# RMSNorm on one core: the first tile's store is cut in two, the last tile's load is put ahead of the second tile's store, and that store goes out as one transfer

## The chip, the cores and the metric

The kernel runs on one core of a Trainium2 chip. The metric is the device time of one execution in microseconds (us); a "span" in a profile is shorter by about 2 us, because it runs from the first to the last instruction. The time before was 162.24 us (median of 3 runs, 161.93 to 162.32).

## The reference

```python
def reference(x, gamma):            # x: 16 x 1024 x 512 float32, gamma: 512 float32
    eps = 1e-5
    rms = np.sqrt(np.mean(x ** 2, axis=-1, keepdims=True) + eps)
    return (x / rms * gamma).astype(np.float32)
```

The input is 33.55 MB and so is the output. Each must cross once between HBM (the memory outside the core) and SBUF (the core's working memory): 67.1 MB in all.

## The kernel before

The 16384 rows are cut into four tiles. In each tile a partition holds R = 32 consecutive rows of 512 floats, 2 KB each, so one tile is 64 KB per partition and 8.4 MB. Three tiles fit into SBUF (`slots`); tile 3 uses slot 0 again, so its load must wait until tile 0 has been stored. All large transfers are issued by the Sync engine (SP), on one queue that feeds 16 DMA engines. ACT (ScalarE) and VectorE (DVE in the profile) compute.

```python
slots = [const.tile([P, R, D], fp32, name=f"slot{i}") for i in range(3)]

def load(t, slot, r0, r1):
    nc.sync.dma_start(out=slots[slot][:, r0:r1], in_=xv[t][:, r0:r1])

def store(t, slot, r0, r1):
    nc.sync.dma_start(out=ov[t][:, r0:r1], in_=slots[slot][:, r0:r1])

load(0, 0, 0, 8)
load(0, 0, 8, 32)
# ... gamma is broadcast to gamma_b; row_stats(slot, g): ACT squares 8 rows,
# ... ACT or VectorE sums them, ACT takes the root, VectorE the reciprocal

def apply(slot, g, rstd):            # VectorE scales 8 rows in place
    for r in range(G):
        nc.vector.scalar_tensor_tensor(
            out=slots[slot][:, g + r, :], in0=slots[slot][:, g + r, :],
            scalar=rstd[:, r : r + 1], in1=gamma_b, op0=OP.mult, op1=OP.mult)

def transfers(t, g):                 # after group g of tile t has been scaled
    if (t, g) == (0, 0):
        store(0, 0, 0, 1)
        load(1, 1, 0, 32)
        load(2, 2, 0, 16)
        store(0, 0, 1, 2)
        load(2, 2, 16, 32)
    elif (t, g) == (0, 24):
        store(0, 0, 2, 32)
    elif (t, g) == (1, 8):
        store(1, 1, 0, 16)
        load(3, 0, 0, 16)
        load(3, 0, 16, 32)
    elif (t, g) == (1, 24):
        store(1, 1, 16, 32)
    elif (t, g) == (2, 24):
        store(2, 2, 0, 32)
    elif (t, g) == (3, 8):
        store(3, 0, 0, 16)
    elif (t, g) == (3, 24):
        store(3, 0, 16, 32)

ahead = row_stats(0, 0)
for k, (t, g) in enumerate(groups):  # statistics run one group ahead
    rstd = ahead
    # ... ahead = row_stats of the next group
    apply(slot_of[t], g, rstd)
    transfers(t, g)
```

## Time and profile before

| what | before |
|---|---|
| time, median of 3 runs | 162.24 us |
| span of the profile | 160.0 us |
| VectorE (DVE) busy | 122.6 us (77%) |
| ACT busy | 80.1 us (50%) |
| share of 16 DMA engines' time, Sync queue | 97.9% |
| first data packet starts, last one ends | 1.7 us, 158.8 us |
| VectorE's last instruction ends, last store is issued | 146.6 us |

The first fence is from the page of the kernel before: busy times, then the span in 40 slices of 4 us (busy tenths, and the GB/s that the DMA engines moved), the DMA queue, and the chain of work that ended last.

```profile
span 160.0 us, 409 instructions
...
PE 2.0 (1%) x2; PEld 0.5 (0%) x2; DVE 122.6 (77%) x163; ACT 80.1 (50%) x162; POOL 0.2 (0%) x4
...
DVE  0101928999999509999999999999999999996000
...
DMA  5999999699699999997999999999996996999993
...
q1 hardware_dynamic: 2160, 67.11, 97.9%
...
DVE 67%; DMA 14%; ACT 7%; issue 2%; DVEq 0%; SPq 0%
```

Two readings compete here. The chain gives VectorE 67%, which looks like a kernel that VectorE bounds. The queue line gives the DMA engines 97.9%. The chain ends in VectorE because the last store is released by VectorE; it does not show that this store then stands in a queue behind other stores. VectorE is at rest in the last slices while DMA is not.

The second fence holds the issues of the Sync engine in the timeline of the kernel before (start, length until the last of the merged issues ends, line, number). L45 is a store and L42 a load. The last row is the last store by itself, which the row above it also counts.

```profile
49.91 23.23 SPq L45 DMA_DIRECT2D out_dram<-slot  x2
...
81.86 1.19 SPq L42 DMA_DIRECT2D slot<-in_x_dram  x2
...
85.73 61.22 SPq L45 DMA_DIRECT2D out_dram<-slot  x4
...
146.62 0.33 SPq L45 DMA_DIRECT2D out_dram<-slot  x1
```

The third is the waits of the Sync engine's own queue: who waited, on what, us in total, times, longest.

```profile
SPq L45 <- DVE slot L88: 120.4, 7, 29.8
...
SPq L42 <- DMA out_dram<-slot: 8.6, 1, 8.6
```

The 8.6 us are the load of tile 3 waiting until tile 0 is stored. The change is aimed at this wait and at where the load stands.

A count can be made from the trace's record of every packet: at each moment, how many of the 16 engines had a packet in flight. I call the missing ones, summed over time and divided by 16, "idle engine time"; a stretch of it between two transfers, when the queue has run dry, is a "hole" ("bubble"). Some packets overlap, by about 0.4 us in all, so the idle time can be understated by as much. For the kernel before it is 0.9 us of 157.1 us between first and last packet: 0.2 us at the start, 0.6 us at the end when the engines finish one after the other, and almost nothing between. A packet of 32 KB takes 1213 ns and one of 64 KB 2418 ns, loads and stores alike.

### The profile page before, as it was taken

To read this page: it belongs to the slowest core of one execution; us is meant where nothing else is said; L and a number is where in the kernel's file an instruction comes from. 1 tells how busy PE (TensorE), PEld (TensorE's weight loads), DVE (VectorE), ACT (ScalarE), POOL (GpSimd) and SP (SyncE) were. 2 spreads that over 40 slices of the span, in tenths; PEclk is the share of its full clock that TensorE was granted. 3 is DMA by queue.
4 is the path that set the end of the run, shared out by engine and by line. 5 is a ranking of instruction groups with operands and counts; after the bars stand their busy time and mean duration, and the time that the engine had idled before them with its cause. 6 is when DMAs were issued, how large, how long until landed. Compare 5 with 4: busy or idle time off the path is not lost.

```text
span 160.0 us, 409 instructions
## 1 busy us (share of the span) xinstructions
PE 2.0 (1%) x2; PEld 0.5 (0%) x2; DVE 122.6 (77%) x163; ACT 80.1 (50%) x162; POOL 0.2 (0%) x4
## 2 busy tenths in 40 slices
PE   4000000000000000000000000000000000000000
PEld 1000000000000000000000000000000000000000
DVE  0101928999999509999999999999999999996000
ACT  3098029991291999996900960069709950000000
POOL 0000000000000000000000000000000000000000
DMA  5999999699699999997999999999996996999993
GB/s 197 524 393 393 430 487 508 279 524 491 295 395 396 456 467 434 494 461 323 445 393 475 426 410 426 475 410 410 491 524 295 508 491 295 467 434 410 426 475 147
DMA packets 2164, 67.13 MB, mean 420 GB/s; under 512 B 241, under 2 KB 241, under 8 KB 498
## 3 DMA queue, kind: packets, MB, share of 16 engines
q1 hardware_dynamic: 2160, 67.11, 97.9%
q14 instruction: 2, 0.02, 0.0%
q10 hardware_dynamic: 2, 0.00, 0.0%
HBM read 33.56 MB, written 33.55 MB: 419 GB/s over the span
## 4 chain that ended last, share of the span: by engine, by line
DVE 67%; DMA 14%; ACT 7%; issue 2%; DVEq 0%; SPq 0%
DVE slot L88 48%; DVE ss L71 18%; DMA slot<-in_x_dram 14%; ACT sq_scratch L76 3%; ACT sq L70 3%; DVE rstd L83 1%; ACT rms L82 1%; DVEq L155 0%; SPq L42 0%
## 5 line engine op out<-in xcount | busy, mean ns | idle before, releaser
L88 DVE SCALAR_TENSOR_TENSOR slot<-slot,rstd,gamma_b 128x512 f32<-128x512 f32 x128 | 85.8, 741 | 0.1
L76 ACT ACTIVATE sq_scratch<-slot 128x512 f32<-128x512 f32 x64 | 40.0, 625 | 10.0 <-DMA slot<-in_x_dram 8.7
L70 ACT ACTIVATE sq<-slot 128x2048 f32<-128x2048 f32 x16 | 29.8, 1865 | 18.8 <-DVE ss L71 11.5
L71 DVE TENSOR_REDUCE ss<-sq 128x4 f32<-128x2048 f32 x16 | 35.9, 2277 | 3.6 <-ACT sq L70 3.6
L82 ACT ACTIVATE rms<-ss,eps_t 128x8 f32<-128x8 f32 x16 | 4.6, 297 | 26.2 <-DVE ss L71 26.0
L83 DVE RECIPROCAL rstd<-rms 128x8 f32<-128x8 f32 x16 | 3.1, 196 | 16.3 <-ACT rms L82 16.3
L76 ACT ACTIVATION_READ_ACCUMULATOR sq_scratch<-slot 128x1 f32 x64 | 11.9, 186 | 0.0
L57 DVE COPY gamma_b<-sq 128x512 f32<-128x512 f32 x1 | 0.7, 691 | 3.3 <-PE sq L55 3.3
L55 PE MATMUL sq<-gamma_row,ones_col 1*128 1x512 f32 x2 | 2.0, 1122 | 2.2 <-DMA gamma_row<-in_gamma_dram 2.2
L76 ACT ACT_TABLE_LOAD x1 | 1.3, 1283 | 1.3 <-PEq L144 1.3
L82 ACT ACT_TABLE_LOAD x1 | 1.3, 1283 | 0.0
L53 DVE MEMSET ones_col<- 1x128 f32 x1 | 0.2, 165 | 0.8 <-PEq L144 0.8
L55 PEld LDWEIGHTS sq<-gamma_row,ones_col 1*128 1x128 f32 x2 | 0.5, 308 | 2.1 <-issue 2.1
L144 POOL MEMSET const-uint8-127<- 128x1 uint8 x1 | 0.1, 102 | 0.0
L144 POOL MEMSET const-bfloat16-1.0<- 128x1 bf16 x1 | 0.1, 101 | 0.0
L144 POOL MEMSET const-float32-0.0<- 128x1 f32 x1 | 0.1, 98 | 0.2 <-issue 0.2
L144 POOL MEMSET const-float32-1.0<- 128x1 f32 x1 | 0.1, 98 | 0.0
L60 DVE MEMSET eps_t<- 128x1 f32 x1 | 0.1, 59 | 0.0
## 6 DMA issues: line engine op xcount, KB each, us to landing
slot<-in_x_dram SPq DMA_DIRECT2D x4, 4096.0 KB, 32.1
out_dram<-slot SPq DMA_DIRECT2D x4, 4096.0 KB, 18.4
out_dram<-slot SPq DMA_DIRECT2D x1, 7680.0 KB
slot<-in_x_dram SPq DMA_DIRECT2D x1, 6144.0 KB, 21.6
slot<-in_x_dram SPq DMA_DIRECT2D x1, 2048.0 KB, 7.2
out_dram<-slot SPq DMA_DIRECT2D x2, 256.0 KB, 21.4
gamma_row<-in_gamma_dram ACTq DMA_DIRECT2D x1, 2.0 KB
slot<-in_x_dram SPq DMA_DIRECT2D x1, 25.9
```

Source lines behind the costliest of these rows:

```text
L53: nc.vector.memset(ones_col, 1.0)
L55: nc.tensor.matmul(gamma_psum[:, 0], ones_col, gamma_row, start=True, stop=True)
L57: nc.vector.tensor_copy(out=gamma_b, in_=gamma_psum[:, 0])
L60: nc.vector.memset(eps_t, eps)
L70: nc.scalar.activation(out=sq, in_=slots[slot][:, g + h : g + h + H, :], func=AF.Square)
L71: nc.vector.tensor_reduce(out=ss[:, h : h + H], in_=sq, axis=mybir.AxisListType.X, op=OP.add)
L76: nc.scalar.activation(out=sq_scratch, in_=slots[slot][:, g + r, :], func=AF.Square, accum_out=ss[:, r : r + 1],)
L82: nc.scalar.activation(out=rms, in_=ss, func=AF.Sqrt, bias=eps_t, scale=1.0 / D)
L83: nc.vector.reciprocal(out=rstd, in_=rms)
L88: nc.vector.scalar_tensor_tensor(out=slots[slot][:, g + r, :], in0=slots[slot][:, g + r, :], scalar=rstd[:, r : r + 1], in1=gamma_b, op0=O ...
L144: nc = _bacc.Bacc("TRN2", target_bir_lowering=False, num_devices=1)
```

## The change

The intent: load tile 3 as early as its slot allows. Tile 0's store is cut in two so that the first half of slot 0 is free while the second half is still being stored; the load of tile 3 follows directly, ahead of all of tile 1's store; tile 1 is then stored in one transfer with 64 KB rows.

```diff
         elif (t, g) == (0, 24):
-            store(0, 0, 2, 32)
-        elif (t, g) == (1, 8):
-            store(1, 1, 0, 16)
+            store(0, 0, 2, 16)
+            store(0, 0, 16, 32)
             load(3, 0, 0, 16)
             load(3, 0, 16, 32)
         elif (t, g) == (1, 24):
-            store(1, 1, 16, 32)
+            store(1, 1, 0, 32)
```

## The prediction

> **What bounds the kernel now.** The DMA engines. The table of DMA queues gives the Sync queue 97.9% of the time of 16 engines. The chain of waits ends in VectorE (67%), but VectorE is done at 146.6 us of a 160.0 us span (timeline). In the trace's packet records the first data packet starts 1.7 us and the last one ends 158.8 us after the start of the span: 157.1 us for 67.1 MB. Counted by packets in flight, the 16 engines lack only 0.9 us (mean of 16), nearly all at the start and in the last microsecond: no bubble in the middle. A 32 KB packet takes 1213 ns and a 64 KB one 2418 ns, loads and stores alike: 27.0 and 27.1 GB/s per engine, 434 GB/s for 16. The Trainium skill, "DMA: Bandwidth & Descriptors", section "Where 436 GB/s comes from", puts the ceiling of the SBUF ports at 435 GB/s; the trace agrees.
>
> **What the change does.** It removes no byte and adds no transfer: store of tile 0 becomes two (28 KB and 32 KB rows), store of tile 1 becomes one (64 KB rows instead of twice 32 KB). 15 transfers on the queue before and after. A 64 KB packet saves 8 ns of 2426, so 8 packets per engine save about 0.06 us. The work of ACT is in the same order; on VectorE one reciprocal in tile 3 moves behind one multiply, which may save 0.26 us.
>
> **Does the new order open a bubble?** As the same page says under "Anatomy of one DMA", waiting is done by the issuing sequencer and not by the DMA engines; what counts is whether the next transfer is issued before the queue runs dry. By the measured rates (us from span start):
> - first half of the remaining store of tile 0: runs 62.3 to about 71; the first load of tile 3 is issued at about 72, while the second half is stored (71 to 80.5). Slack 7 us.
> - second load of tile 3: issued at about 82 (as before, 81.9 to 83), while the first is running (80.5 to 90). Slack 7 us.
> - store of tile 1: waits for VectorE's end of tile 1 at 85.7; its turn is at about 100. Slack 14 us.
> - store of tile 2: issued at 115.9, turn at about 119.5, as before. The two of tile 3: issued at 131.5 and 146.6, turns at about 138.5 and 148.2, as before. The last has the least slack, some 0.5 us (issue to first packet took 1.0 us at the start).
>
> Tile 3 lands about 10 us earlier (about 90 and 100 instead of 100 and 110), but ACT first wants it at about 106, and the waits show no DMA wait after 43 us. So it releases nothing. The Sync queue's wait on tile 0's store (8.6 us) becomes two, some 22 and 9 us, both behind queued transfers.
>
> **Prediction.** 162.2 us, range 161.7 to 162.7. Faster by over 2%: 1%; within 2%: 98%; slower: 1%.
>
> **What would show it.** Right: Sync queue again near 98%, mean near 420 GB/s, last packet about 157 us after the first, VectorE's end at 146 to 147 us, no ACT wait on a load after 45 us, packet times unchanged. Wrong: a slice in which fewer than 16 packets are in flight near 72, 82, 100 or 148 us, or 64 KB stores slower than 2.42 us.
>
> **What would make it wrong.** VectorE ending later by over half a microsecond, or reads and writes beside each other slowing packets.

## More of the kernel before

Whether a wait of the Sync engine costs time depends on whether the DMA engines still have work queued meanwhile. The windows view of the kernel before answers that for the two critical moments (columns: window, its length, busy us of PE, PEld, DVE, ACT and POOL with counts, PE clock, DMA share, GB/s).

```profile
80.00:82.00 2.00, 0.00 (x0) 0.00 (x0) 2.00 (x5) 0.17 (x2) 0.00 (x0) 1.00 1.10 475
...
146.00:150.00 4.00, 0.00 (x0) 0.00 (x0) 0.59 (x1) 0.00 (x0) 0.00 (x0) 1.00 1.08 467
```

Both windows show full engines. (A packet's bytes and time are not spread evenly over short windows, so a share can pass 1; only a share near 0 means an empty queue.)

## The result

Changed: 162.12 us median (161.80 to 162.32, 4 runs); before in the same rounds: 162.18 us (161.93 to 162.32, 4 runs). The ratio is 0.9996, 95% interval 0.9975 to 1.0017: the same. A ratio here is the mean time of one kernel's fast runs over the mean of the other's fast runs of the same rounds, so it is not quite the ratio of the medians quoted beside it. A later repeat (below) gave 1.0006, interval 0.9981 to 1.0030.

The page of the changed kernel:

```profile
span 160.4 us, 410 instructions
...
PE 2.0 (1%) x2; PEld 0.5 (0%) x2; DVE 122.6 (76%) x163; ACT 80.1 (50%) x162; POOL 0.2 (0%) x4
...
DVE  0100928999999519999999999999999999994000
...
DMA  5999999699699999999999999998998998999993
...
q1 hardware_dynamic: 2160, 67.11, 97.7%
...
DVE 67%; DMA 13%; ACT 7%; issue 2%; DVEq 0%; SPq 0%
```

Its Sync issues in the timeline, again with the last store in a row of its own:

```profile
49.81 0.34 SPq L45 DMA_DIRECT2D out_dram<-slot  x1
...
72.22 10.13 SPq L42 DMA_DIRECT2D slot<-in_x_dram  x2
...
85.63 60.96 SPq L45 DMA_DIRECT2D out_dram<-slot  x4
...
146.25 0.33 SPq L45 DMA_DIRECT2D out_dram<-slot  x1
```

Its Sync waits and the two windows:

```profile
SPq L45 <- DVE slot L88: 97.9, 7, 29.8
SPq L42 <- DMA out_dram<-slot: 31.3, 2, 21.9
```

```profile
80.00:82.00 2.00, 0.00 (x0) 0.00 (x0) 2.00 (x5) 0.08 (x1) 0.00 (x0) 1.00 1.03 442
...
146.00:150.00 4.00, 0.00 (x0) 0.00 (x0) 0.23 (x1) 0.00 (x0) 0.00 (x0) 1.00 1.05 451
```

The issues moved as intended: the first load of tile 3 is issued at 72.2 us instead of 81.9. The Sync engine now waits 31.3 us on stores instead of 8.6, and it costs nothing, since the queue is full throughout: idle engine time is 1.3 us (0.3 at the start, 0.9 at the end, nothing between). VectorE's last result comes 0.4 us earlier (the last store is issued at 146.25 instead of 146.62) and the profile's span is 0.4 us longer: a small sign that VectorE's end is not what sets the time. Between first and last packet there are 157.5 us (157.1 before).

### The profile page after: what moved, and what is told of

It is laid out like the page before. It is cut to its first block, busy times and chain, and to the rows that moved or that the text cites. A ratio compares the mean times of both kernels' runs of the same rounds, so it can differ in the third digit from the quotient of the medians.

```text
span 160.4 us, 410 instructions
## 1 busy us (share of the span) xinstructions
PE 2.0 (1%) x2; PEld 0.5 (0%) x2; DVE 122.6 (76%) x163; ACT 80.1 (50%) x162; POOL 0.2 (0%) x4
## 4 chain that ended last, share of the span: by engine, by line
DVE 67%; DMA 13%; ACT 7%; issue 2%; DVEq 0%; SPq 0%
DVE slot L88 48%; DVE ss L71 18%; DMA slot<-in_x_dram 13%; ACT sq_scratch L76 3%; ACT sq L70 3%; DVE rstd L83 1%; DVEq L154 0%; ACT rms L82 0%; SPq L42 0%
```

## The experiments

The theory: the 16 DMA engines are busy from the first packet to the last, so the order and the size of the transfers are free as long as each next transfer is issued before the queue runs dry; the change keeps to that before and after. The rivals: two parts of the change that cancel; VectorE as the bound, as the chain suggests; the landing time of tile 3 as what matters.

This table, worked out from the packet records of each profile, is used throughout. "Packet time" is the sum of all packets' durations over 16. First-to-last is about packet time plus idle time, less the 0.4 us of overlap. The labels belong to these experiments: e3 to 1, e7 to 2, e5 to 3, e6 to 4, e4 to 5, e1 and f3 to 6, e2 to 7, f1 and f2 to 8, g1 to 9, g2 to 10.

```
kernel                        first to last   idle engine time   packet time   (us)
before                            157.1             0.9             156.6
changed                           157.5             1.3             156.6
g2_after_again                    157.8             1.6             156.5
e3_move_alone                     157.1             0.9             156.6
e7_load_late                      157.3             1.2             156.5
e5_no_apply                       156.8             0.6             156.6
f2_tail_8rows                     157.3             1.1             156.6
g1_fewer_turns                    157.4             0.7             156.9
e6_late_vector                    159.4             2.9             156.9
e4_last_whole                     165.1             8.8             156.6
f1_tail_2rows                     159.9             1.7             158.6
e1_unsplit                        161.1             3.0             158.5
f3_unsplit_again                  160.9             3.1             158.2
e2_merge_alone                    164.6             6.5             158.4
```

### 1. The move without the large store

```diff
+        elif (t, g) == (1, 8):
+            store(1, 1, 0, 16)
         elif (t, g) == (1, 24):
-            store(1, 1, 0, 32)
+            store(1, 1, 16, 32)
```

> The changed kernel with tile 1 stored in two halves of 32 KB rows, as before the change; the load of tile 3 stays between the stores. Theory: 162.1 us (161.8 to 162.5), the same within 0.2%, since no part of the change does anything. Rival (two effects of opposite sign cancel in the change: the earlier load wins, the one large store loses, or the other way round): a difference of more than 0.3% from both kernels.

Measured: 162.00 us, before 161.86; ratio 1.0013 (1.0001 to 1.0026). The theory said the same within 0.2%, and the interval stays under the rival's 0.3%. The two parts of the change do not hide opposite effects: the earlier load alone is worth nothing either.

### 2. The load of tile 3 made later

```diff
 (kernel before)
         elif (t, g) == (1, 8):
             store(1, 1, 0, 16)
-            load(3, 0, 0, 16)
-            load(3, 0, 16, 32)
         elif (t, g) == (1, 24):
             store(1, 1, 16, 32)
+            load(3, 0, 0, 16)
+            load(3, 0, 16, 32)
```

> The kernel before with the load of tile 3 put behind the second half of tile 1's store: tile 3 lands near 110 and 120 us, 10 us later than before and 20 us later than in the changed kernel. Theory: ACT waits some 4 to 5 us for the load at 106 to 110 us, but VectorE has 10 us of other work there, so it ends within 1 us of 146.5 us and the last store still finds the queue full: 162.1 us (161.8 to 162.7). Rival (when tile 3 lands matters): 4 us or more above 162.2.

Measured: 161.85 us, before 161.86; ratio 1.0006 (0.9993 to 1.0018). The load does come late enough to be waited for; the waits of this kernel show it:

```profile
ACT sq_scratch L76 <- DMA slot<-in_x_dram: 14.1, 3, 5.5
```

The same line of the kernel before:

```profile
ACT sq_scratch L76 <- DMA slot<-in_x_dram: 8.7, 2, 5.4
```

So one wait of about 5.4 us is new, where 4 to 5 were expected. Still the time is the same: VectorE had other work meanwhile and ended at 146.8 us, and the queue stayed full. Tile 3 may land some 20 us apart in two kernels (this one and the changed one) without any effect.

### 3. No work on VectorE's side of the stores

```diff
 (changed kernel; the output is x unscaled, wrong on purpose)
-        apply(slot_of[t], g, rstd)
```

> The changed kernel without the scaling (the output is x unchanged, wrong on purpose): no store waits for VectorE, which loses 86 of its 123 us of work. Theory: the DMA engines still have the same 67.1 MB to move: 162.1 us (161.6 to 162.4), first data packet to last about 157 us. Rival (VectorE, 67% of the chain of waits, sets the pace): clearly faster, below 155 us.

Measured: 161.48 us, before 162.15; ratio 0.9965 (0.9950 to 0.9980). It missed the stated range by 0.1 us on the fast side, far from the rival's 155. With VectorE's busy time cut to a third the kernel gains 0.35%:

```profile
span 159.6 us, 280 instructions
...
PE 2.0 (1%) x2; PEld 0.5 (0%) x2; DVE 39.4 (25%) x35; ACT 79.4 (50%) x162; POOL 0.2 (0%) x4
...
q1 hardware_dynamic: 2160, 67.11, 98.2%
```

That is the strongest evidence against reading the chain's 67% as the bound. In this profile the engines finished within 0.7 us of each other, against 0.95 us before and 1.3 us in the changed kernel. Whether that explains the 0.35% is open.

### 4. VectorE late at the end

```diff
 (changed kernel; pad is a tile that nobody reads)
+        if (t, g) == (3, 24):
+            for _ in range(6):
+                nc.vector.scalar_tensor_tensor(
+                    out=pad, in0=slots[0][:, 31, :], scalar=rstd[:, 0:1],
+                    in1=gamma_b, op0=OP.mult, op1=OP.mult)
         apply(slot_of[t], g, rstd)
```

> The changed kernel with six further VectorE multiplies of 128x512 (to a tile nobody reads) in the last group of tile 3, 4.0 us of work at 0.66 us each. Theory: the last store had a slack of some 1.3 us on the mean of the engines (issue at 146.4 plus 1.0 us, the engines dry at 148.3 to 149.2), so 4.0 us late costs 2.6 us: 164.7 us (164.2 to 165.3). Rival (VectorE sets the pace): the full 4.0 us, 166.1. Rival (VectorE never matters): 162.1.

Measured: 164.34 us, before 162.15; ratio 1.0139 (1.0119 to 1.0158), that is 2.2 us for 4.0 us of work. The theory said 2.6 and its range held. In the packet records a hole of 2.6 us stands ahead of the last store. Of it 0.5 us or more is given back at the end: after the hole all engines start the last store together and finish within 0.16 us, so the uneven finish of 0.9 us in the changed kernel is gone. VectorE thus has a slack of about 1.4 us (4.0 less the hole of 2.6) ahead of the last store, and beyond it it does set the time. "Not the bound" does not mean "free".

### 5. The last tile's store made whole

```diff
 (changed kernel)
-        elif (t, g) == (3, 8):
-            store(3, 0, 0, 16)
         elif (t, g) == (3, 24):
-            store(3, 0, 16, 32)
+            store(3, 0, 0, 32)
```

> The changed kernel with the last tile, instead of only tile 1, stored as one transfer of 64 KB rows once all of it is scaled. Theory: the engines finish the store of tile 2 at about 138.8 us on the mean and have nothing until VectorE ends at 146.4 and 1.0 us of issue have passed: a bubble of 8.6 us, 170.8 us (170.2 to 171.5). Rival (a transfer of 64 KB rows is as good wherever it stands, or VectorE sets the pace and the last store is only short of its own length): no more than 4 us above.

Measured: 169.80 us, before 162.15; ratio 1.0473 (1.0456 to 1.0491), 7.7 us more. The same merge that cost nothing in tile 1 costs 5% here, because nothing stands queued in front of it. Windows of this kernel:

```profile
132.00:138.00 6.00, 0.00 (x0) 0.00 (x0) 6.00 (x8) 0.30 (x1) 0.00 (x0) 1.00 0.86 371
140.00:142.00 2.00, 0.00 (x0) 0.00 (x0) 2.00 (x4) 0.00 (x0) 0.00 (x0) 1.00 0.00 0
142.00:144.00 2.00, 0.00 (x0) 0.00 (x0) 2.00 (x4) 0.00 (x0) 0.00 (x0) 1.00 0.00 0
144.00:146.00 2.00, 0.00 (x0) 0.00 (x0) 2.00 (x4) 0.00 (x0) 0.00 (x0) 1.00 0.00 0
148.00:156.00 8.00, 0.00 (x0) 0.00 (x0) 0.00 (x0) 0.00 (x0) 0.00 (x0) 1.00 0.91 393
```

A DMA share of 0.00 while VectorE is fully busy is what a dry queue looks like. The forecast was 8.6 us. The hole measures 8.4 us, and the even finish after it gives back some 0.7 us, as in experiment 4. That term was missing in the forecast. (The hole is 0.2 us shorter than forecast: this store's first packet came 0.83 us after its issue, not 1.0.)

### 6. The move without the cut in tile 0's store

This is the changed kernel with tile 0 stored as one piece. In a first draft the scheduler put tile 1's store back ahead of the load, which made the order of transfers that of experiment 7; so here the store is tied behind the load (`load` returns its instruction for that).

```diff
 (changed kernel)
-            store(0, 0, 2, 16)
-            store(0, 0, 16, 32)
+            store(0, 0, 2, 32)
             load(3, 0, 0, 16)
-            load(3, 0, 16, 32)
+            last_load.append(load(3, 0, 16, 32))
         elif (t, g) == (1, 24):
-            store(1, 1, 0, 32)
+            with tc.issue_after(last_load[0].ins):
+                store(1, 1, 0, 32)
```

> The changed kernel with the store of tile 0 in one piece (rows 2 to 31), the order of the queue held otherwise. Theory (the DMA engines are always busy; only a queue run dry costs time): the first load of tile 3 must wait for the whole store, with nothing queued behind it. The wait ends near 81.9 us, first packet 1.0 us later, while the engines fall idle at 80.4 to 81.3 us: a bubble of about 2.0 us on the mean, and 164.2 us (163.8 to 164.7), with VectorE ending at about 146.4 us as before. Rival (what is at work is the earlier load of tile 3 or the one large store of tile 1, which this kernel has too): 162.1 us. Rival (VectorE sets the pace, since the chain of waits gives it 67%): 162.1 us.

Measured: 165.76 us, before 161.86; ratio 1.0238 (1.0223 to 1.0254), 3.9 us more, where 2.0 were expected (a miss in size). A second profile of the same kernel was taken to see whether the excess is stable:

> The first experiment's kernel once more, for a second profile of it: 165.7 us (165.4 to 166.0). If the slow packets are a property of that order, they show again at the same two places: over 0.3 us (mean of 16 engines) after the bubble and over 0.7 us where the load of tile 3 ends; if they were chance, elsewhere or less.

Measured: 165.82 us, before 161.82; ratio 1.0248. The windows view of experiment 6 shows two weak spots:

```profile
72.00:80.00 8.00, 0.00 (x0) 0.00 (x0) 8.00 (x12) 6.47 (x16) 0.00 (x0) 1.00 0.92 399
80.00:82.00 2.00, 0.00 (x0) 0.00 (x0) 2.00 (x5) 0.37 (x2) 0.00 (x0) 1.00 0.00 0
...
90.00:98.00 8.00, 0.00 (x0) 0.00 (x0) 8.00 (x15) 4.90 (x12) 0.00 (x0) 1.00 0.93 401
98.00:104.00 6.00, 0.00 (x0) 0.00 (x0) 6.00 (x7) 0.00 (x0) 0.00 (x0) 1.00 1.03 350
```

At 80 to 82 us the share is 0.00: the hole, 2.2 us of idle engine time, as expected. At 98 to 104 us the engines count as busy but move only 350 GB/s: packets that last longer. The packet records say by how much. After the hole the first load packets took up to 2.1 us instead of 1.2; where the load of tile 3 ends and tile 1's store begins, the last load packets took up to 2.2 us. Added up over all engines and divided by 16:

```
                     packets begun after the hole   last packets of the load of tile 3
e1_unsplit                    0.57 us                        1.3 us
f3_unsplit_again              0.50 us                        1.3 us
changed (no hole)             none                           0.13 us
```

So 2.2 us of hole plus 1.9 us of slow packets, less some 0.3 us of more even finish, make up the 3.9 us. The repeat shows both places again. The cut in tile 0's store is thus the one part of the change that is needed: without it the move would have cost 2.4%.

### 7. The large store without the move

```diff
 (kernel before)
-        elif (t, g) == (1, 8):
-            store(1, 1, 0, 16)
+        elif (t, g) == (1, 24):
+            store(1, 1, 0, 32)
             load(3, 0, 0, 16)
             load(3, 0, 16, 32)
-        elif (t, g) == (1, 24):
-            store(1, 1, 16, 32)
```

> The kernel before with only one part of the change: tile 1 stored in one transfer once all of it is scaled, still ahead of the load of tile 3. Theory: the engines run dry at about 80.9 us on the mean and get the store of tile 1 only after VectorE's end of tile 1 at 85.7 us, first packet 86.7: a bubble of 5.8 us. Tile 3 lands near 116 and 126 us, so ACT waits some 10 us for it and VectorE ends 5 to 6 us later (about 152), still in time for the last store at about 154. Total 168.0 us (167.4 to 168.8): the bubble alone counts, the later VectorE doesn't add. Rival (larger transfers are worth something by themselves): under 162.2 us. Rival (the landing time of the load decides): VectorE's delay adds to the bubble, above 172 us.

Measured: 169.42 us, before 161.86; ratio 1.0472 (1.0457 to 1.0487), 7.6 us more. The hole of 5.8 us came as forecast, VectorE ended at 153.0 us without adding to it, and the whole is 0.6 us above the stated range. The missing amount is again in slow packets (packet time 158.4 us instead of 156.6). They are not right after the hole, where stores follow stores (0.08 us), but at the next two changes of direction: 0.8 us at the end of tile 1's store ahead of the load, 1.0 us at the end of the load ahead of tile 2's store.

Put together: in experiments 4 and 5 a hole was followed by stores only, and no packets were slow (0.04 us). In experiments 6 and 7 a hole was followed by changes between loads and stores, and these cost about 2 us. In the kernels without a hole the same changes cost 0.2 us or less from 70 us on. The length of the hole hardly matters: from 70 us on the slow packets add up to 2.0, 1.9, 1.9 and 1.9 us behind holes of 1.0 (experiment 8), 2.2 and 2.3 (experiment 6, two profiles) and 5.8 us.

### 8. How small the second piece of tile 0's store may be

Experiment 6's order, with the cut at row 30 and at row 24 in place of none.

```diff
 (experiment 6)
-            store(0, 0, 2, 32)
+            store(0, 0, 2, 30)       # f2_tail_8rows: 24 in place of 30
+            store(0, 0, 30, 32)
```

> The first experiment's order (forced), with the store of tile 0 cut as rows 2 to 29 and rows 30 to 31: the wait of tile 3's first load ends one small transfer (0.6 us of queue) earlier, at about 80.9 us, first packet 0.95 us later, while the engines run dry at 80.7 to 81.5 us: a bubble of 0.7 to 1.0 us. The first experiment cost 1.9 us more than its bubble of 2.1 us; its trace has those 1.9 us in packets that took longer than usual (the first ones after the bubble, and the last loads ahead of tile 1's store). If a restart from a dry queue brings that cost whatever its length: 164.0 us (163.2 to 165.0) with a second stretch of slow packets worth over 0.5 us (mean of 16 engines) where the load of tile 3 ends. If the slow packets were chance or belong to long bubbles: 162.9 (162.5 to 163.2).

> The same with the cut at row 24: 8 rows, 2.4 us of queue, stand behind what the load waits for. Landing to first packet is about 1.5 us (0.5 from the last completion to issue, 0.95 from issue to packet) and the engines' spread 0.8 us, so no bubble: 162.1 us (161.7 to 162.5), no slow stretch beyond the one of about 0.1 to 0.2 us in the changed kernel. If a bubble is there after all, 163 or more.

Measured with 2 rows: 164.57 us, before 161.82; ratio 1.0168 (1.0155 to 1.0181). The hole was 1.0 us, and slow packets stood again in both places (0.56 us after the hole, 1.4 us where the load ends). The cost of restarting does not shrink with the hole. With 8 rows: 161.91 us, before 161.82; ratio 1.0010 (0.9997 to 1.0023), no hole and no such slow packets. The two expectations have the queue's length wrong by a factor of two: by the packet records the two rows kept each engine busy for 1.3 us (not 0.6) and the eight rows for 4.9 us (not 2.4). Both forecasts of the hole held all the same: the first was reckoned from the times at which the engines had run dry, and eight rows are enough by either figure. What has to be covered is about 2.3 us: 1.5 us from the end of the last packet waited for to the first new one (0.5 us until the issue, 0.95 us from issue to packet) and the 0.8 us by which the engines finish apart. The two rows fall short of that by the 1.0 us of the hole; eight rows cover it twice, and the half tile in the change four times.

### 9. Fewer changes of direction

The slow packets suggested a version that might beat both kernels: drop the two stores of a single row at the beginning.

```diff
 (changed kernel)
     load(0, 0, 8, 32)
+    load(1, 1, 0, 32)
+    load(2, 2, 0, 16)
+    load(2, 2, 16, 32)
 ...
-        if (t, g) == (0, 0):
-            store(0, 0, 0, 1)
-            load(1, 1, 0, 32)
-            load(2, 2, 0, 16)
-            store(0, 0, 1, 2)
-            load(2, 2, 16, 32)
-        elif (t, g) == (0, 24):
-            store(0, 0, 2, 16)
+        if (t, g) == (0, 24):
+            store(0, 0, 0, 16)
             store(0, 0, 16, 32)
```

> The changed kernel without the two stores of a single row of tile 0: the loads of tiles 1 and 2 are issued straight after tile 0's, and tile 0 is stored as rows 0 to 15 and 16 to 31. The queue then turns from loads to stores and back three times fewer. In all profiles so far the last packets of a load ahead of such a small store were slow, by 0.3 us (mean of 16 engines) at 20 to 22 us and 0.05 to 0.35 us at 48 to 52 us; load after load never was. Theory (a busy queue is all that counts, and turns are the small rest): 161.6 us against 162.0, ratio 0.995 to 0.999, no bubble. Rival (these small stores are of use, for instance by spreading the engines): 162.0 us or more.

Measured: 162.53 us, before 161.82; ratio 1.0038 (1.0013 to 1.0062). This guess failed. The slow packets ahead of the small stores are gone, but the first real change from loads to stores, at 58 to 62 us, now has 1.1 us of them (in one profile), more than all those it replaced (0.7 us in the changed kernel, at 18 to 22 and 48 to 52 us; 0.6 to 0.9 us between 10 and 64 us in all thirteen profiles that have the two small stores). The profile accounts for some 0.3 us of the 0.6 us lost; it is of the fastest of the six runs (162.21 us). (The expectation counts three turns less; there are four, two there and two back.) Windows of this kernel, then of the kernel before:

```profile
52.00:56.00 4.00, 0.00 (x0) 0.00 (x0) 2.00 (x1) 4.00 (x4) 0.00 (x0) 1.00 1.14 492
56.00:62.00 6.00, 0.00 (x0) 0.00 (x0) 2.60 (x4) 5.78 (x18) 0.00 (x0) 1.00 1.00 350
```

```profile
52.00:56.00 4.00, 0.00 (x0) 0.00 (x0) 2.28 (x2) 3.88 (x4) 0.00 (x0) 1.00 1.07 456
56.00:62.00 6.00, 0.00 (x0) 0.00 (x0) 2.32 (x3) 5.78 (x18) 0.00 (x0) 1.00 1.03 437
```

It is the signature of experiment 6's second spot: busy engines at 350 GB/s. So the cost belongs not to every change of direction: after the start it falls on the early ones, and with small stores there it is lower. After a restart the runs can't tell the first changes from later ones: experiment 6 has one change after the first new packets and experiment 7 two, and each of them was slow. A possible mechanism is that engines that start together change direction together and get in each other's way, and drift apart afterwards. This is argued, not shown: the engines' spread does not order the cases cleanly.

### 10. The changed kernel again

> The changed kernel again, beside the kernel before, for a narrower interval. Theory: ratio 0.998 to 1.002 with 1.000 inside the interval.

Measured: 161.96 us, before 161.82; ratio 1.0006 (0.9981 to 1.0030). No difference is shown. The profile is of the slowest of the six runs (162.44 us): of its 1.6 us of idle engine time 1.3 are the uneven finish, against 0.9 in the first profile of the same program. So the finish alone differs by 0.4 us between two runs of one kernel.

## Why the prediction was right

- **The bound.** It named the DMA engines and not VectorE, against the chain of waits. Experiment 3 shows it: VectorE's busy time cut from 122.6 to 39.4 us gains 0.35%.
- **The rate.** The prediction compared the engines' rate with the Trainium skill's 435 GB/s. The skill's "HBM Reference", section "Specifications (TRN2)", says that a core streaming alone measures about 425 GB/s, bounded by its 16 DMA engines. This agrees: 67.1 MB in 157.1 us are 427 GB/s. Whether the engines themselves, their ports or the memory set the time of a packet, no run here tests; the argument needs only that they are never without one.
- **What the change is worth.** It was forecast as no bytes and no transfers less. The packet times are unchanged (1213 and 2418 ns) and the packet time is 156.6 us in both. The 0.06 us for larger packets is too small to be seen.
- **Slack.** Each transfer was forecast to be issued before its turn. The issues came at 72.2, 82, 85.6 and 146.25 us, as forecast within half a microsecond, and no hole appears. Experiments 5, 6 and 7 show that a missing slack would have been seen: they cost 2.4% to 4.7%. The slack of the last store was called 0.5 us, by the first engine to finish; on the mean of the engines experiment 4 gives 1.4 us.
- **The earlier load releases nothing.** Experiment 1 (early, nothing else) and experiment 2 (later than before) give the same time.
- **The Sync engine's waits.** They were forecast as two waits of 22 and 9 us in place of one of 8.6; measured were 31.3 us in two, the longest 21.9. As the skill says in "DMA: Bandwidth & Descriptors", "Anatomy of one DMA — SWDGE (gpsimd) path", where it speaks of the DMA engines in general, the sequencer waits and the DMA engines do not. The trace agrees: they ran through these waits at full rate.

What later forecasts had wrong were sizes, in terms that the prediction had no need of: a dry queue costs more than its length when loads follow or loads and stores change places afterwards (1.9 us of slow packets in experiment 6), and less when only stores follow (0.5 us or more given back by the even finish), and a small transfer keeps the queue busy twice as long as was reckoned (experiment 8).

## What to carry to other kernels

When the DMA engines are full from the first packet to the last, moving transfers about and merging them gained nothing here; ask of a reordering first whether the queue could run dry, and compare the issue time of each transfer with the time of its turn. A transfer that must wait for another one's landing needs other work queued behind that one, here some 2.3 us by an estimate from experiment 8 (1.3 us of it left a hole of 1.0 us, 4.9 us left none): cut the earlier transfer rather than leave it whole. The skill's "Perfetto Trace Analysis", section "DMA Optimizations", says that splitting may help if DMA engines are generally idle; here they are not idle, and the cut was still necessary, to keep them so.

## What the Trainium skill lacked or had wrong

- "DMA: Bandwidth & Descriptors", "Where 436 GB/s comes from", says that for transfers between HBM and SBUF the HBM side (about 358 GB/s) binds. On this one core it did not: 427 GB/s from first to last packet, and 434 GB/s by the packets' own duration. The passage itself sets beside it a 16 MB transfer measured at 425 GB/s, and the "HBM Reference" has it right for a core alone; the sentence lacks the condition.
- No page that I found tells what a dry queue costs beyond its length. Here a hole of 1.0 us cost 2.7 us and one of 2.2 us cost 3.9, about 1.9 us of each in packets of 1.2 us that took up to 2.3 us right after the hole and where loads and stores change places; after a hole that only stores follow there were next to none (0.04 us).
- No page that I found tells that the first change from loads to stores is dear: 1.1 us with large transfers only (one profile), 0.6 to 0.9 us for all the early changes together when two stores of one row each are among them (thirteen profiles).
- "DMA: Bandwidth & Descriptors", "Specifications", gives about 0.6 us to the first byte for transfers issued by Sync or ACT. On an empty queue it was 0.95 to 1.0 us here from the start of the issue instruction to the first packet of a load, and 0.83 to 0.84 us to that of a store (experiments 4, 5 and 7); 0.33 to 0.38 us of it is the issue itself, so the page agrees, with 0.5 to 0.6 us, if it counts from the issue's end. From the end of the last packet waited for to the next issue it took another 0.5 us.
